# Weight subtractions of the state-space and router stage moved from GpSimd to Vector, gates computed directly behind the slot matrices

## The chip, the core and the metric

The kernel runs on one core of one Trainium2 chip. The metric is the device time of one execution in microseconds (us). Five engines work side by side, each through its own list of instructions in order: TensorE (PE: matrix products; PEld is its loading of weights), VectorE (DVE), ScalarE (ACT), GpSimd (POOL) and SyncE (SP), which here only issues transfers. An instruction waits for others by semaphores, and whatever stands behind it on its engine waits with it.

## The reference

Two decoder layers over 256 tokens with D = 1024, everything in float32. Layer 0 is attention and a dense SwiGLU. The change lies in layer 1: a state-space layer with a gated output, then a router that sends each token to two of eight expert SwiGLUs.

```python
def _s5_layer(x, norm_g, w_in, ...):
    u = _rms_norm(x, norm_g) @ w_in
    ...                                   # complex diagonal scan over the tokens, giving y
    z = gelu(y + d_skip * u) @ w_glu
    return x + z[..., :D_MODEL] * sigmoid(z[..., D_MODEL:])

def _moe_swiglu_layer(x, norm_g, w_router, w_gate, w_up, w_down):
    xt = _rms_norm(x, norm_g)
    logits = xt @ w_router
    top_vals, top_idx = lax.top_k(logits, 2)
    gates = softmax(top_vals)
    ...                                   # gather the tokens of each expert
    y_e = (silu(xb @ w_gate[e]) * (xb @ w_up[e])) @ w_down[e]
    return x + sum over the two experts of gate * y_e
```

## The kernel before, in words

**Weights.** Almost all of the time goes into large products with weights that come from memory in blocks. For most of them each float32 factor is split into a rounded part (high) and what is left (low), and a product is made of three matmuls: high by high, high by low, low by high (`mm3`, L248, its matmuls on L250 to L252). A weight block of 128x2048 arrives in a raw buffer in two halves of 128x1024. `half()` (L207) prepares one: ScalarE casts it to `wh` (L221), then one subtraction `wl = raw - wh` (L222) follows on the engine that `self.sub` names, or that the caller gives. The pair (wh, wl) lies in a ring of six slots, of which one is given up at L1445, so that five are left for the rest of the kernel. `take` and `takek` (L233, L244) hand pairs to the matmuls and make new ones so many ahead. When both halves of a raw buffer are split, `drop` returns the buffer, and `fetch` issues the next block's transfer on SyncE's queue (L184, L187). So a subtraction also sets when the next block may start to arrive. Experts 1, 3, 5 and 7 have at most 64 tokens; their products read the raw weights in plain float32 (L717, L751) and need no pairs.

**Order.** There is no scheduler in this part: each engine runs its instructions in the order in which the Python code emits them. In `s5_and_moe` (L1206) this is:

1. `s5_rows` gives the rows transposed and their sums of squares; `rsqrt` (L255 to L276) makes the norm factor `r` on Vector by a chain of tiny operations; the line behind it sets `self.sub = nc.gpsimd`, and `takek` makes two more pairs.
2. `project` multiplies by w_in. The eviction by ScalarE (L1230) takes `r` as its scale, and Vector transposes the result into the layout for the states (L1231); `enter` (L1274) is the next product on it. `chain` is the scan on Vector, a few of its products are on GpSimd (L1256).
3. `glu` (L1345) multiplies by w_glu; `gate(n)` (L1392, its sigmoids on L1395) and `residual(n, b)` (L1397) form h + z * sigmoid(z') for column half n and token block b; `rows` (L1403) forms `xn`, the rows times the gain; `rows_T` (L1407) transposes them on TensorE and ScalarE copies them out (L1412); `logits` (L1418) adds a column half's share of the router's logits.
4. The half n = 1 ends the stage: `self.split()` (two halves of weights, on GpSimd), the residuals, the transposes, the logits, then `squares` (L333, on ScalarE over whole rows, for the second norm factor) and one more `self.half(nc.gpsimd)`.
5. The router on Vector: maximum and index (L1477, L1478), `sel` (one-hot choice), `ss`, two small matmuls for the places, `posm` (L1485).
6. `experts` (L1603) runs a list of steps for expert 0. Step 0 makes the slot matrix `S` (L1579); `rows_rest` makes `xn` of column half 1 and drops the buffer "sa"; `weights` (L1493) is the second rsqrt and the two sigmoids of the top two logits, the gates; steps 2 and 3 gather the tokens by a product with `S` (L1598) and evict it (ScalarE L1600, then a subtraction on Vector). The first expert's products follow. At its fourth chunk `count()` (L1507) runs on Vector: some 25 tiny operations that order the experts by their number of tokens.

The helper `tt` (L1210) records every plain Vector operation of this stage, so these share one line and are told apart by tiles: `h` residual, `sg`/`gh` gates, `xn` rows, `sel` choice, `wy` evicted tokens.

Of the kernel before, what the change touches and what calls it, by code (L numbers as in the profile page):

```python
# [8 lines left out]
F32 = mybir.dt.float32  # L9
# [4 lines left out]
AF = mybir.ActivationFunctionType  # L14
ALU = mybir.AluOpType
# [3 lines left out]
P = 128  # L19
SEQ = 256  # L20
D = 1024
# [119 lines left out]
class Net:  # L141
# [185 lines left out]
    def squares(self, scr, act):  # L327

        nc = self.nc
        ssq = self.sm.tile([P, 2], F32, tag="ssq", name="ssq")  # L330
        for b in range(2):
            if b in act:
                nc.scalar.activation(scr[b], self.h[:, b], AF.Square, accum_out=ssq[:, b:b + 1])  # L333
            else:
                nc.vector.scalar_tensor_tensor(out=scr[b], in0=self.h[:, b], scalar=1.0, in1=self.h[:, b], op0=ALU.mult, op1=ALU.mult,
                                               accum_out=ssq[:, b:b + 1])
        return ssq
# [868 lines left out]
    def s5_and_moe(self):  # L1206
        nc, tc, ins = self.nc, self.tc, self.ins
        mm = nc.tensor.matmul
        v = nc.vector
        tt = lambda o, a, b, op: v.tensor_tensor(out=o, in0=a, in1=b, op=op)  # L1210
# [4 lines left out]
        xh, xl, ssq = self.srows  # L1215
        tt(ssq[:, 0], ssq[:, 0], ssq[:, 1], ALU.add)
        r = self.rsqrt(ssq[:, 0], 2, 1.0 / D)
        self.sub = nc.gpsimd
        W = self.takek(4, 1) + self.takek(4, 1)


# [170 lines left out]
        def gate(n):  # L1392
            for b in range(2):
                sg[b] = self.two(("sg", "gh")[b], 0)
                nc.scalar.activation(sg[b], pz[n, 1, b], AF.Sigmoid)  # L1395

        def residual(n, b, o=0, w=512):  # L1397
            c = slice(512 * n + o, 512 * n + o + w)
            s = sg[b][:, o:o + w]
            tt(s, s, pz[n, 0, b][:, o:o + w], ALU.mult)  # L1400
            tt(self.h[:, b, c], self.h[:, b, c], s, ALU.add)

        def rows(n, b):  # L1403
            c = slice(512 * n, 512 * n + 512)
            tt(xn[:, b, c], self.h[:, b, c], gb[:, c], ALU.mult)

        def rows_T(n, b, js=range(4)):  # L1407
            pt = pgu.tile([P, 4, P], F32, tag="gu", name="hpt")
            for j in js:
                k = 4 * n + j  # L1410
                nc.tensor.transpose(pt[:, j], self.h[:, b, k * P:(k + 1) * P], self.ident)
            nc.scalar.copy(hT[:, 4 * n + js[0]:4 * n + js[-1] + 1, blk[b]], pt[:, js[0]:js[-1] + 1])  # L1412
# [3 lines left out]
        def logits(n, b, js=range(4)):  # L1416
            for k in range(4 * n + js[0], 4 * n + js[-1] + 1):
                mm(pl[b], hT[:, k, blk[b]], self.wrg[:, k], start=(k == 0), stop=(k == KD - 1))  # L1418

        gate(0)  # L1420
        Wg.append(self.takek(4, 1))
        for b in range(2):
# [6 lines left out]
            rows_T(0, b)  # L1429
        for b in range(2):  # L1430
            logits(0, b)
        gate(1)
        Wg.append(self.takek(4, 1))
        glu(1, 0, 0, range(4))
# [8 lines left out]

        self.ahead = 4
        self.drop(self.ring.pop(0))  # L1445
        self.split()
        residual(1, 0)
        rows_T(1, 0)
        for o in range(2):
            pz[1, 0, 1] = last[o]  # L1450
            residual(1, 1, 256 * o, 256)
            rows_T(1, 1, range(2 * o, 2 * o + 2))
        for b in range(2):
            logits(1, b)
        self.sub = v
        ssq = self.squares([self.sa[:, 0]] * 2, (0, 1))
        self.half(nc.gpsimd)


        iota = self.cst[:, C_IO:C_IO + P + 1]  # L1460
# [31 lines left out]

        def weights():  # L1493

            r = self.rsqrt(ssq, 2, 1.0 / D)
            nc.scalar.activation(self.sm.tile([P, 1], F32, tag="cf", name="cf"), self.ones[:, 0:1], AF.Sigmoid)
            v.tensor_copy(GR[:, NE], r)
            dg = mo.tile([P, 2, 2], F32, name="dg")
            tt(dg[:, 0], mx[:, :, 0], mx[:, :, 1], ALU.subtract)
            tt(dg[:, 0], dg[:, 0], r, ALU.mult)  # L1500
            nc.scalar.activation(dg[:, 1], dg[:, 0], AF.Sigmoid, scale=-1.0)
            nc.scalar.activation(dg[:, 0], dg[:, 0], AF.Sigmoid)
            for s in range(2):
                tt(sel[:, s], sel[:, s], dg[:, s].unsqueeze(2).to_broadcast([P, 2, NE]), ALU.mult)
            tt(GR[:, 0:NE].rearrange("p e b -> p b e"), sel[:, 0], sel[:, 1], ALU.add)
# [205 lines left out]

            self.ffn([job(e) for e in range(NE)], g1, pgu)

        def rows_rest():
            for b in range(2):
                rows(1, b)
            self.drop((self.sl, "sa"))

        experts((0, rows_rest, weights, 2, 3), True)

        def over():

# [80 lines left out]
```

## Time and profile before

| | us |
|---|---|
| median of three runs (1299.54 to 1300.69) | 1299.7 |
| the profiled execution | 1299.78 |
| its span on the core | 1297.7 |
| TensorE busy | 1263.9 |
| VectorE busy | 829.0 |
| ScalarE busy | 634.9 |
| GpSimd busy | 205.2 |

The span runs from the first to the last instruction of the core; 2.1 us of the profiled execution lie around it. The mean granted clock of TensorE is 0.992 of full speed. All times below count from the start of the span; the stage of the change lies between 376 and 470 us. A row of the timeline gives start, duration, engine, line, operation, out<-in with sizes, the number of instructions taken together, and in brackets the idle time just before and what ended it. A row of the windows gives for a stretch its length and each engine's busy time with the number of instructions, then the granted clock, the share of the 16 DMA engines' time and the rate. A row of the groups gives the number, the busy time and the mean ns of one.

### The profile page before, as it was taken

To read this page: it belongs to the slowest core of one execution; us is meant where nothing else is said; L and a number is where in the kernel's file an instruction comes from. 1 tells how busy PE (TensorE), PEld (TensorE's weight loads), DVE (VectorE), ACT (ScalarE), POOL (GpSimd) and SP (SyncE) were. 2 spreads that over 40 slices of the span, in tenths; PEclk is the share of its full clock that TensorE was granted. 3 is DMA by queue.
4 is the path that set the end of the run, shared out by engine and by line. 5 is a ranking of instruction groups with operands and counts; after the bars stand their busy time and mean duration, and the time that the engine had idled before them with its cause. 6 is when DMAs were issued, how large, how long until landed. Compare 5 with 4: busy or idle time off the path is not lost.

```text
span 1297.7 us, 18489 instructions
## 1 busy us (share of the span) xinstructions
PE 1263.9 (97%) x6862; PEld 918.6 (71%) x6862; DVE 829.0 (64%) x1102; ACT 634.9 (49%) x825; POOL 205.2 (16%) x295
## 2 busy tenths in 40 slices
PE   8999999999998799999999999999999999999997
PEld 8867999999987688863458884356886345888433
DVE  7876869666777699861079982138985107998201
ACT  6665544444443378751067771046875106777100
POOL 1841994012815400000000000000000000000000
PEclk9999999999999799999999999999999999999999
DMA  8504653654446569999999999999999999999996
GB/s 313 215 7 176 250 180 136 218 182 176 162 163 247 224 246 376 359 369 393 420 418 417 417 419 413 420 417 417 418 418 418 419 418 418 418 418 418 414 419 239
DMA packets 66370, 421.23 MB, mean 325 GB/s; under 512 B 7504, under 2 KB 8784, under 8 KB 21472
## 3 DMA queue, kind: packets, MB, share of 16 engines
q1 hardware_dynamic: 65088, 418.15, 81.1%
q10 hardware_dynamic: 1008, 1.27, 0.3%
q8 instruction: 56, 0.92, 0.3%
q0 software_dynamic: 176, 0.56, 0.1%
q14 instruction: 42, 0.34, 0.1%
HBM read 418.89 MB, written 1.05 MB: 324 GB/s over the span
## 4 chain that ended last, share of the span: by engine, by line


## 5 line engine op out<-in xcount | busy, mean ns | idle before, releaser
L222 DVE TENSOR_TENSOR wl<-raw,wh 128x1024 fp32r<-128x1024 f32 (+1 forms) x445 | 533.5, 1235 | 103.1 <-ACT wh L221 90.3
L221 ACT CAST wh<-raw 128x1024 fp32r<-128x1024 f32 (+1 forms) x456 | 467.5, 1046 | 177.7 <-PE dn L252 62.7
L717 PE MATMUL pgu<-raw,we 128*64 128x512 f32 x896 | 203.6, 596 | 0.0
L250 PE MATMUL pgu<-wh,wy 128*128 128x512 f32 x448 | 178.2, 398 | 0.0
L251 PE MATMUL pgu<-wl,wy 128*128 128x512 f32 x448 | 174.7, 390 | 0.6 <-DVE wl L222 0.6
L252 PE MATMUL pgu<-wh,wy 128*128 128x512 f32 x448 | 174.8, 390 | 0.0
L717 PEld LDWEIGHTS pgu<-raw,we 128*64 128x64 f32 x896 | 61.0, 137 | 115.5 <-issue 114.0
L250 PE MATMUL pgu<-dxh,wh 128*128 128x256 f32 x448 | 127.3, 284 | 0.5 <-DVE h L679 0.5
L252 PE MATMUL pgu<-dxh,wl 128*128 128x256 f32 x448 | 126.8, 283 | 0.0
L251 PE MATMUL pgu<-dxl,wh 128*128 128x256 f32 x448 | 126.8, 283 | 0.0
L250 PE MATMUL dn<-wh,gh 128*128 128x512 f32 x280 | 109.8, 392 | 0.0
L252 PE MATMUL dn<-wh,gl 128*128 128x512 f32 x280 | 109.1, 390 | 0.0
L251 PE MATMUL dn<-wl,gh 128*128 128x512 f32 x280 | 109.0, 389 | 0.0
L751 PE MATMUL dn<-raw,gh 128*64 128x512 f32 x448 | 102.2, 593 | 0.5 <-ACT gh L737 0.5
L250 PEld LDWEIGHTS pgu<-wh,wy 128*128 128x128 f32 x448 | 84.2, 188 | 23.8 <-issue 4.7
L252 PEld LDWEIGHTS pgu<-wh,wy 128*128 128x128 f32 x448 | 84.1, 188 | 18.2
L251 PEld LDWEIGHTS pgu<-wl,wy 128*128 128x128 f32 x448 | 84.2, 188 | 17.4 <-DVE wl L222 1.0
L737 ACT COPY gh<-pgt 128x256 f32<-128x256 f32 x28 | 10.4, 372 | 163.7 <-PE pgt L735 163.7
L728 DVE TENSOR_TENSOR sg<-pgu,sg 64x512 f32<-64x512 f32 x28 | 19.4, 693 | 110.9 <-ACT sg L727 110.9
L250 PEld LDWEIGHTS pgu<-dxh,wh 128*128 128x128 f32 x448 | 85.9, 192 | 1.1 <-DVE h L679 0.7
L251 PEld LDWEIGHTS pgu<-dxl,wh 128*128 128x128 f32 x448 | 86.0, 192 | 0.3
L252 PEld LDWEIGHTS pgu<-dxh,wl 128*128 128x128 f32 x448 | 85.9, 192 | 0.0
(419 smaller groups left out, 1615.9 us busy)
## 6 DMA issues: line engine op xcount, KB each, us to landing
raw<-in_wm_dram SPq DMA_DIRECT2D x292, 1024.0 KB, 15.0
raw<-in_wm_dram SPq DMA_DIRECT2D x88, 512.0 KB, 15.0
raw<-in_wd_dram SPq DMA_DIRECT2D x42, 1024.0 KB, 5.0
raw<-in_wqkv_dram SPq DMA_DIRECT2D x6, 1024.0 KB, 6.6
raw<-in_wo_dram SPq DMA_DIRECT2D x4, 1024.0 KB, 5.9
raw<-in_wglu_dram SPq DMA_DIRECT2D x4, 1024.0 KB, 5.0
raw<-in_ws_dram SPq DMA_DIRECT2D x2, 1024.0 KB, 4.7
raw<-in_wc_dram SPq DMA_DIRECT2D x4, 416.0 KB, 6.7
```

The source lines that it names most:

```text
L221: self.nc.scalar.copy(wh, w)
L222: (sub or self.sub).tensor_tensor(out=wl, in0=w, in1=wh.bitcast(F32), op=ALU.subtract)
L250: mm(out, sh, mh, start=start, stop=False)
L251: mm(out, sh, ml, start=False, stop=False)
L252: mm(out, sl, mh, start=False, stop=stop)
L717: nc.tensor.matmul(pg[64 * j:64 * j + 64], x(k), W[j][0][k % 4], start=(k == 0), stop=(k == KD - 1))
L728: v.tensor_tensor(out=sg[:64], in0=pg[64:], in1=sg[:64], op=ALU.mult)
L737: nc.scalar.copy(g, pt)
L751: nc.tensor.matmul(job["acc"][64 * n:64 * n + 64], gts[0][:, k], W[n][0][k], start=(f == 0 and k == 0), stop=(f == NF - 1 and k == 3))
```

## The change

- `self.sub = nc.gpsimd` is deleted, so every subtraction `wl` of the stage goes to Vector, at the place in the order where `half()` is called: two directly behind the first rsqrt, four in front of `residual(0, ...)`, two in front of `residual(1, ...)`.
- The explicit `self.split()` in front of `residual(1, 0)` and the `self.half(nc.gpsimd)` behind the squares are removed. In their place three `self.half` stand in the first expert's list of steps: behind step 0, behind step 2 and behind step 3. The number of pairs that are made before the first expert's fourth chunk stays the same.
- The squares for the second norm factor are made in column halves on ScalarE: half 0 behind `logits(0, ...)` and in front of `gate(1)`, half 1 behind `logits(1, ...)`. `weights` adds the two sums first.
- `xn` of column half 1 is made in front of `logits(1, ...)`, not behind `S`; the buffer "sa" is dropped directly behind the second half of the squares.
- `weights` stood behind `rows_rest` and in front of step 2 and now stands behind one `half` and in front of step 2.

```diff
@@ s5_and_moe
         r = self.rsqrt(ssq[:, 0], 2, 1.0 / D)
-        self.sub = nc.gpsimd
         W = self.takek(4, 1) + self.takek(4, 1)
...
+        ssq = self.sm.tile([P, 2, 2], F32, tag="ssq4", name="ssq4")
+
+        def squares(n):
+            c = slice(512 * n, 512 * n + 512)
+            for b in range(2):
+                nc.scalar.activation(self.sa[:, 0, c], self.h[:, b, c], AF.Square, accum_out=ssq[:, n, b:b + 1])
+
         gate(0)
...
         for b in range(2):
             logits(0, b)
+        squares(0)
         gate(1)
         Wg.append(self.takek(4, 1))
         glu(1, 0, 0, range(4))
...
         self.drop(self.ring.pop(0))
-        self.split()
         residual(1, 0)
         rows_T(1, 0)
...
         for b in range(2):
+            rows(1, b)
+        for b in range(2):
             logits(1, b)
-        self.sub = v
-        ssq = self.squares([self.sa[:, 0]] * 2, (0, 1))
-        self.half(nc.gpsimd)
+        squares(1)
+        self.drop((self.sl, "sa"))
...
         def weights():
-            r = self.rsqrt(ssq, 2, 1.0 / D)
+            tt(ssq[:, 0], ssq[:, 0], ssq[:, 1], ALU.add)
+            r = self.rsqrt(ssq[:, 0], 2, 1.0 / D)
...
-        def rows_rest():
-            for b in range(2):
-                rows(1, b)
-            self.drop((self.sl, "sa"))
-
-        experts((0, rows_rest, weights, 2, 3), True)
+        experts((0, self.half, weights, 2, self.half, 3, self.half), True)
```

The lines of the changed kernel are one lower than before from L1219 on, and up to eight higher from the new function on.

The first place is Vector's list behind the first rsqrt (the last two rows of its chain, then the transposes of the projection; `sg` and `gx` are the evicted projections, `sa` their transposed form).

```order
 L271 SCALAR_TENSOR_TENSOR rt<-rr,rm 128x1 x2
 L276 SCALAR_TENSOR_TENSOR rr<-rt,rr 128x1 x2
-L1231 STREAM_TRANSPOSE sa<-sg 128x8x32
-L1231 STREAM_TRANSPOSE sa<-gx_4140 128x8x32
-L1231 STREAM_TRANSPOSE sa<-sg 128x8x32
+L222 TENSOR_TENSOR wl<-raw,wh 128x1024 x2
+L1230 STREAM_TRANSPOSE sa<-sg 128x8x32
+L1230 STREAM_TRANSPOSE sa<-gx_4140 128x8x32
+L1230 STREAM_TRANSPOSE sa<-sg 128x8x32
```

Two subtractions of weights now stand on Vector between the norm factor and the transposes.

The second place is Vector's list in the router, from the last choice to the start of the second rsqrt (`posm` the places, `S` the slot matrix, `rx` the first tile of the rsqrt).

```order
 L1210 TENSOR_TENSOR ss<-sel 128x16
-L1485 SCALAR_TENSOR_TENSOR posm<-dn_4697,ss 128x16
-L1579 TENSOR_SCALAR S<-cst,posm 128x128 x2
-L1210 TENSOR_TENSOR xn<-h,sa 128x512 x2
-L259 TENSOR_SCALAR rx<-ssq 128x2
+L1492 SCALAR_TENSOR_TENSOR posm<-dn_4689,ss 128x16
+L1587 TENSOR_SCALAR S<-cst,posm 128x128 x2
+L222 TENSOR_TENSOR wl<-raw,wh 128x1024
+L1210 TENSOR_TENSOR ssq_4513<-ssq_4513 128x2
+L259 TENSOR_SCALAR rx<-ssq_4513 128x2
```

The two `xn` have gone to a place further ahead, and one weight subtraction and the sum of the squares stand between `S` and the rsqrt.

The third place is ScalarE's list from the copies of the transposed rows (half 0) to the cast behind the squares, before:

```order
L1412 COPY wy_4509<-hpt 128x4x128 x2
L1395 ACTIVATE sg<-dn_4533 128x512
L1395 ACTIVATE gh<-dn_4546 128x512
L221 CAST wh<-raw 128x1024 x4
L1412 COPY wy_4509<-hpt 128x4x128
L1412 COPY wy_4509<-hpt 128x2x128 x2
L333 ACTIVATE sa,ssq<-h 128x1024 x2
L221 CAST wh<-raw 128x1024
```

and now:

```order
L1411 COPY wy_4509<-hpt 128x4x128 x2
L1424 ACTIVATE sa,ssq_4513<-h 128x512 x2
L1394 ACTIVATE sg<-dn_4534 128x512
L1394 ACTIVATE gh<-dn_4547 128x512
L221 CAST wh<-raw 128x1024 x2
L1411 COPY wy_4509<-hpt 128x4x128
L1411 COPY wy_4509<-hpt 128x2x128 x2
L1424 ACTIVATE sa,ssq_4513<-h 128x512 x2
L221 CAST wh<-raw 128x1024
```

Two squares of half width now stand ahead of the gates, two casts fewer stand behind them, and the squares behind the copies are half as wide.

## The prediction

> **What bounds the kernel now.** I read the busy line of the page first, then windows around the stage, then the groups of L222, then the timeline at each place where TensorE stands still.
>
> ```profile
> PE 1263.9 (97%) x6862; PEld 918.6 (71%) x6862; DVE 829.0 (64%) x1102; ACT 634.9 (49%) x825; POOL 205.2 (16%) x295
> core 0: us, PE busy (x) PEld busy (x) DVE busy (x) ACT busy (x) POOL busy (x), PEclk, DMA share, GB/s
> 386.00:407.00 21.00, 16.21 (x160) 14.42 (x160) 20.71 (x46) 4.89 (x7) 10.30 (x14) 1.00 0.41 154
> 411.00:425.00 14.00, 14.00 (x66) 11.56 (x65) 7.04 (x7) 6.99 (x10) 10.09 (x4) 1.00 0.89 329
> 434.20:439.70 5.50, 1.49 (x8) 1.08 (x9) 4.92 (x5) 1.33 (x3) 4.70 (x2) 0.82 0.85 337
> 439.70:443.20 3.50, 3.44 (x18) 3.38 (x17) 0.43 (x4) 3.20 (x6) 0.00 (x0) 0.50 1.00 332
> 447.10:452.70 5.60, 5.60 (x33) 5.60 (x33) 4.61 (x25) 0.88 (x3) 0.00 (x0) 0.62 0.53 187
> 452.70:463.00 10.30, 9.72 (x51) 7.79 (x49) 7.54 (x32) 7.49 (x9) 0.00 (x0) 1.00 0.28 103
> 600.00:700.00 100.00, 99.07 (x472) 53.40 (x472) 45.26 (x49) 38.22 (x48) 0.00 (x0) 1.00 1.01 418
> ```
>
> TensorE is busy 97% of the span, so only its gaps and slow stretches can go. Vector sets the pace in 386 to 407 (20.71 of 21). In 434.2 to 439.7 TensorE works 1.49 of 5.5 while Vector and GpSimd are both almost full. The next stretch runs at a granted clock of 0.50.
>
> ```profile
> L222 DVE TENSOR_TENSOR wl<-raw,wh 128x1024 fp32r<-128x1024 f32 x10 | 11.7, 1218 | 1.2 <-ACT wh L221 1.2
> L222 POOL TENSOR_TENSOR wl<-raw,wh 128x1024 fp32r<-128x1024 f32 x11 | 27.5, 2524 | 43.9 <-PE dn L252 25.8 <-ACT wh L221 18.1
> ```
>
> Eleven subtractions, 2.52 us each on GpSimd, 1.22 us on Vector. The question is what Vector's own work loses while GpSimd makes one.
>
> **First rsqrt, and the two subtractions behind it.**
>
> ```profile
> 377.13 2.46 DVE L276 SCALAR_TENSOR_TENSOR rr<-rt,ri 128x1 f32<-128x1 f32 x2
> 377.18 4.75 POOL L222 TENSOR_TENSOR wl<-raw,wh 128x1024 fp32r<-128x1024 f32 x2 [25.80 <-PE dn L252]
> 379.51 2.56 DVE L271 SCALAR_TENSOR_TENSOR rt<-rr,rm 128x1 f32<-128x1 f32 x2
> 382.69 0.47 ACT L1230 ACTIVATE sg<-dn,rr 128x256 f32<-128x256 f32 x1 [4.64 <-DVE rr L276]
> 384.14 1.97 PE L1274 MATMUL pe<-sa,we 128*128 128x128 f32 x16 [1.21 <-issue]
> 449.98 0.27 DVE L276 SCALAR_TENSOR_TENSOR rr<-rt,rr 128x1 f32<-128x1 f32 x2
> ```
>
> Operations on one column, 0.27 us a pair at 449.98 with GpSimd idle, take 2.46 and 2.56 while GpSimd subtracts. Without that r is ready 4.5 earlier, at 382.69 - 4.5 = 378.2. The two subtractions then stand ahead of the transposes: 378.2 + 2 x 1.22 = 380.7. From the end of ScalarE's eviction (383.16) to TensorE's start lie 1.0, mostly transposes, so they are done at 381.7. TensorE works until 384.14 - 1.21 = 382.93 and then goes on at once: **-1.2**. The chain behind it fills Vector and nothing is added there, so the gain carries through; were Vector's chain held up by something the trace doesn't show, the gain would be 0.
>
> **Residual of half 0, with four subtractions ahead.**
>
> ```profile
> 417.74 2.00 ACT L221 CAST wh<-raw 128x1024 fp32r<-128x1024 f32 x2
> 425.19 1.03 PE L1411 MATMUL hpt<-cst,h 128*128 128x128 f32 x8
> ```
>
> The last cast ends at 419.74; the third subtraction starts at 418.75, the fourth ends at 421.2, and then come two products (0.7 each) and two adds (0.65) to 423.9. TensorE wants h at 425.19 and is full in 411 to 425, so this costs **0** with 1.3 us of cover. If the adds stay at 2.1, as some do beside GpSimd now, it costs about 1.6.
>
> **Residual of half 1.**
>
> ```profile
> 427.74 2.96 ACT L221 CAST wh<-raw 128x1024 fp32r<-128x1024 f32 x3
> 431.38 0.69 DVE L1210 TENSOR_TENSOR sg<-sg,pz 128x512 f32<-128x512 f32 x1 [4.96 <-PE pz L1345]
> 432.11 2.11 DVE L1210 TENSOR_TENSOR h<-h,sg 128x512 f32<-128x512 f32 x1
> 434.58 2.13 DVE L1210 TENSOR_TENSOR h<-h,gh 128x256 f32<-128x256 f32 x1
> 437.07 2.12 DVE L1210 TENSOR_TENSOR h<-h,gh 128x256 f32<-128x256 f32 x1
> 439.24 0.69 PE L1411 MATMUL hpt<-cst,h 128*128 128x128 f32 x2 [1.98 <-DVE h L1210]
> 440.24 1.06 ACT L333 ACTIVATE sa<-h 128x1024 f32<-128x1024 f32 x1
> 447.13 1.29 DVE L1210 TENSOR_TENSOR xn<-h,sa 128x512 f32<-128x512 f32 x2
> ```
>
> Three adds take 2.1 each, whether 512 or 256 wide; a clean one of 512 takes 1.29 / 2 = 0.65, and I take 0.35 for 256. Ahead of them stands more now: squares(0) delays ScalarE by about 1.3 (two of half width, 0.53 each by the row of the full one, and 0.2 for reading the sums), so the first cast runs from 429.1 to 430.1, the second to 431.1. Two subtractions follow, to 432.6, instead of the start at 431.38. Then 0.69 + 0.65 + 0.41 + 0.35 + 0.41 + 0.35 = 2.9, with 0.2 of gaps: 435.7 instead of 439.24, **-3.5**. On SyncE the transfers that waited for GpSimd's subtractions wait for Vector's, which end earlier.
>
> **Logits.**
>
> ```profile
> 426.46 1.95 PE L1418 MATMUL dn<-kp,wy 128*128 128x8 f32 x16 [0.24 <-ACT wy L1412]
> 439.72 3.42 PE L1418 MATMUL dn<-kp,wy 128*128 128x8 f32 x16
> ```
>
> The same sixteen matmuls take 1.95 at full clock and 3.42 in the stretch at 0.50, which follows 5.5 us with 1.49 of work. With the adds shortened, the last gap shrinks to under 2 us and the stretch is about 60% busy, so I take full clock: **-1.5**, or 0 if it still drops. The two xn, now ahead of the logits on Vector, take 1.3 while TensorE makes these logits: nothing.
>
> The Trainium skill, "TensorE: Matmul & The Clock Gate", Part 1, says that the clock goes to half after an idle window of about 3.4 us and back after a busy one. The row shows 0.50 behind a stretch that was never idle for that long (1.49 of 5.5 busy), so the trace is harsher than the rule; by the rule the term is -1.5, by the row alone it may be 0.
>
> **Router, and the gather.**
>
> ```profile
> 443.67 2.36 DVE L1210 TENSOR_TENSOR sel<-cst,ix 128x16 f32<-128x16 f32 x2
> 447.08 5.85 PE L1598 MATMUL dn<-S,xn 128*128 128x128 f32 x32 [0.59 <-DVE S L1579]
> 448.34 0.16 DVE L259 TENSOR_SCALAR rx<-ssq 128x2 f32<-128x2 f32 x1
> 451.22 0.26 DVE L1210 TENSOR_TENSOR sel<-sel,dg 128x16 f32<-128x16 f32 x2 [0.51 <-ACT dg L1502]
> 451.70 0.69 DVE L1210 TENSOR_TENSOR wy<-dn,wy 128x512 fp32r<-128x512 f32 x1
> 456.63 0.15 DVE L1590 COPY gs<-dn 128x2 f32<-128x2 f32 x1
> 461.70 6.90 DVE L222 TENSOR_TENSOR wl<-raw,wh 128x1024 fp32r<-128x1024 f32 x6
> 462.99 0.50 PE L251 MATMUL pgu<-wl,wy 128*128 128x512 f32 x1 [0.58 <-DVE wl L222]
> ```
>
> `sel` takes 2.36 beside GpSimd's last subtraction, a like pair 0.26 alone: **-2.1**. So the gather starts 1.2 + 3.5 + 1.5 + 2.1 = 8.3 earlier, at 438.8.
>
> From there to the seventh weight pair, the first that TensorE waits for, it is now 462.99 - 447.08 = 15.9. After: 0.1, one subtraction 1.2, the sum of the squares 0.2, rsqrt and gates 3.4 (448.34 to 451.70), eviction 0.7: 5.6; then 0.4 for a cast, 1.2, the second eviction 0.7, 1.2, and the sixth pair 1.2: 10.3. `count()` takes 5.1 (456.63 to 461.70) and the seventh subtraction 1.2: 16.6. **+0.7** (0 if TensorE's own work up to that pair, 15.1 before its wait, gets longer by as much; +2.9 if a cast waits for a ring slot and comes late with its subtraction, 1.0 + 1.2, since the evictions and all of `count()` are queued behind it on Vector).
>
> **The sum.** -1.2 + 0 - 3.5 - 1.5 - 2.1 + 0.7 = -7.6. Does it reach the end? From 600 on the transfers fill the DMA engines (1.01, 418 GB/s), so the stream must start earlier as well.
>
> ```profile
> SPq L187 <- DVE wl L222: 29.8, 10, 7.9
> ```
>
> It can: in 452.7 to 463 the share is 0.28, and this row, SyncE's waits between 430 and 500, says that its issues stand behind Vector's subtractions. These shift with the stage, and the stream with them. The profiled execution becomes 1299.78 - 7.6 = 1292.2; it lies 0.08 over the median, so the forecast is **1292.1**. That the gates now come "in front of the evictions" adds nothing: `weights` stood ahead of step 2 before.
>
> **The rivals.**
>
> *The clock still drops in the router.* For it: 0.50 behind a stretch that was partly busy. Against: a shorter gap. 1292.1 + 1.5 = **1293.6**, chance 0.15.
>
> *Vector's queue is the bound in the first expert*, by a cast that waits for a slot: +2.9 instead of +0.7, **1294.3**; chance 0.06. Against: one slot of the five is free each time TensorE ends a pair, and the cast has been early so far (1.2 us of waiting in all for ten subtractions).
>
> *The stream of weights does not move*, because the last bytes are bound from further ahead: **1299.7**, no change; chance 0.08. Against: the share of 0.28.
>
> *Slower: the stalls are not GpSimd's.* If the tiny operations and the adds stay long for a reason of their own, the subtractions come on top of Vector's path: two ahead of the transposes, 382.69 + 2.4 to start them instead of 383.2, +1.9; the residual 432.6 instead of 431.38, +1.1; and +0.7. That is +3.7: **1303.4**, chance 0.05. It decides from the point where the rsqrt chain without GpSimd still takes over about 4 us. Against it: 0.27 at 449.98.
>
> The Trainium skill, "Perfetto Trace Analysis", Optimizing Scalar/DVE Operations, speaks against the change: where Vector is saturated, offloading to Scalar or even GpSimd may make sense, though it adds that Vector and GpSimd share a read port, so it might not help. Here 11 x 1.22 = 13.4 us go onto Vector, but none falls into the one stretch that is full (20.71 of 21), so the rule would cost its 13.4 only if that were so everywhere.
>
> **How the numbers follow.** Forecast 0.66, clock 0.15, queue 0.06, stream 0.08, slower 0.05. Faster than 0.2% (2.6 us, about what a measurement of this kernel can tell from no change) holds the first three: 0.87; same 0.08; slower 0.05. The range goes from 1289.5 to 1296.0. Its lower end is the forecast without the +0.7 and with the residual's start not put off by the squares (431.4 instead of 432.6), 1290.2, less 0.7 for the spread of runs; its upper end is the clock and the queue together, 1295.8. It leaves out 0.13 and a little of the forecast's own spread.
>
> **What would show it.** In the profile of the changed kernel: L276 and L271 behind the first rsqrt at 0.3 a pair and no gap of 1.21 ahead of L1273; adds of half 1 at 0.65 and 0.35; the last transposes at about 434.5; the logits at 1.95 with a clock of 1.00; `sel` at 0.26; the gather at 438.8 and the seventh pair 16.6 behind it; no subtraction on GpSimd. I am wrong if adds stay near 2.1 with GpSimd idle, if the last weights land no earlier than now, or if the seventh pair comes later than 18 behind the gather.

## The result and the profile after

The changed kernel took 1290.07 us (median of four runs, 1289.86 to 1291.47) against 1299.62 for the kernel before: ratio 0.993, 95% interval 0.9914 to 0.9946. A second set of five runs, beside 21 of the kernel before, gave 1291.43 against 1299.55, ratio 0.9932 (0.9918 to 0.9945). The span of the profiled execution went from 1297.7 to 1288.1.

The busy line of the page and the group of Vector's subtractions between 374 and 462 us, after:

```profile
PE 1260.8 (98%) x6862; PEld 915.1 (71%) x6862; DVE 826.5 (64%) x1114; ACT 635.4 (49%) x829; POOL 178.2 (14%) x284
L222 DVE TENSOR_TENSOR wl<-raw,wh 128x1024 fp32r<-128x1024 f32 x23 | 27.0, 1220 | 8.9 <-ACT wh L221 8.9
```

GpSimd lost its eleven subtractions (27 us). Vector made them at 1.22 each, 13.4 in all, and is yet 2.5 us less busy than before: what it took on is less than what it had spent held up.

The timeline after the first rsqrt:

```profile
377.50 0.27 DVE L276 SCALAR_TENSOR_TENSOR rr<-rt,ri 128x1 f32<-128x1 f32 x2
378.61 2.36 DVE L222 TENSOR_TENSOR wl<-raw,wh 128x1024 fp32r<-128x1024 f32 x2
381.25 0.40 DVE L1230 STREAM_TRANSPOSE sa<-gx 128x256 f32<-128x256 f32 x1
383.15 1.90 PE L1273 MATMUL pe<-sa,we 128*128 128x128 f32 x16
```

The small operations take 0.27 a pair, the two subtractions stand behind them, and TensorE's row has no idle time in brackets any more. The rest of the stage, from the residual of half 1 to the seventh weight pair:

```profile
427.52 2.36 DVE L222 TENSOR_TENSOR wl<-raw,wh 128x1024 fp32r<-128x1024 f32 x2 [5.17 <-ACT wh L221]
429.80 0.68 DVE L1210 TENSOR_TENSOR sg<-sg,pz 128x512 f32<-128x512 f32 x1
430.51 0.69 DVE L1210 TENSOR_TENSOR h<-h,sg 128x512 f32<-128x512 f32 x1
431.57 0.42 DVE L1210 TENSOR_TENSOR h<-h,gh 128x256 f32<-128x256 f32 x1
432.36 0.42 DVE L1210 TENSOR_TENSOR h<-h,gh 128x256 f32<-128x256 f32 x1
433.12 1.93 PE L1417 MATMUL dn<-kp,wy 128*128 128x8 f32 x16
435.57 0.26 DVE L1210 TENSOR_TENSOR sel<-cst,ix 128x16 f32<-128x16 f32 x2
436.53 0.48 DVE L1587 TENSOR_SCALAR S<-cst,posm 128x128 f32<-128x128 f32 x2
436.87 6.07 PE L1606 MATMUL dn<-S,xn 128*128 128x128 f32 x32 [0.59 <-DVE S L1587]
444.55 2.36 DVE L222 TENSOR_TENSOR wl<-raw,wh 128x1024 fp32r<-128x1024 f32 x2 [0.15 <-ACT wh L221]
446.82 0.15 DVE L1598 COPY gs<-dn 128x2 f32<-128x2 f32 x1
451.91 6.90 DVE L222 TENSOR_TENSOR wl<-raw,wh 128x1024 fp32r<-128x1024 f32 x6
453.19 0.50 PE L251 MATMUL pgu<-wl,wy 128*128 128x512 f32 x1 [0.80 <-DVE wl L222]
```

The adds take 0.69 and 0.42, the logits 1.93, the choice 0.26; the gather stands at 436.87 (438.8 was foretold) and the seventh pair 16.3 behind it.

Executions reach this stage up to 1.4 us apart, so two profiles are compared from one mark: the sum of the squares on Vector (`ssq<-ssq`, at 376.19 before and 376.56 after). The table counts every start from it, except for the end of the last add. It is made from the timeline of each profile, and the later kernels stand in it too; the last column is TensorE's first product for the output (`po<-Y,ST`), 1288.77 before and 1279.07 after.

| | first product on the transposed input | transposes, half 0 | last add, its end | gather | seventh pair | output product |
|---|---|---|---|---|---|---|
| before | 7.95 | 49.00 | 63.00 | 70.89 | 86.80 | 912.58 |
| before, second profile | 7.95 | 48.75 | 62.74 | 70.63 | 86.21 | 912.30 |
| after | 6.59 | 45.94 | 56.22 | 60.31 | 76.63 | 902.51 |
| after, second profile | 6.59 | 47.52 | 58.96 | 62.98 | 79.05 | 905.18 |
| all subtractions on Vector, old order | 6.58 | 45.92 | 59.45 | 67.07 | 83.00 | 908.71 |
| new order, eight on GpSimd | 7.95 | 48.99 | 60.32 | 65.16 | 81.22 | 907.08 |
| first two on GpSimd | 7.95 | 47.39 | 57.68 | 61.69 | 78.30 | 904.55 |
| last two on GpSimd | 6.58 | 45.97 | 57.29 | 62.56 | 79.32 | 905.23 |
| three idle two-input operations | 6.57 | 45.93 | 60.12 | 65.92 | 82.83 | 909.01 |
| one of these, eight idle memsets | 6.59 | 45.94 | 57.92 | 63.71 | 79.83 | 906.04 |
| half ahead of the router on GpSimd | 6.57 | 47.57 | 57.86 | 63.68 | 80.68 | 906.58 |
| gates first | 6.57 | 47.55 | 57.82 | 61.83 | 78.28 | 904.30 |

From the sum of the squares to the output product the first pair of profiles differs by 912.58 - 902.51 = 10.07, the second by 912.30 - 905.18 = 7.12. What differs between the two profiles of the changed kernel is the granted clock, below.

### The profile page after: what moved, and what is told of

Same layout as the page of the kernel before. It is cut to its first block, busy times and chain, and to the rows that moved or that the text cites. A ratio compares the mean times of both kernels' runs of the same rounds, so it can differ in the third digit from the quotient of the medians.

```text
span 1288.1 us, 18482 instructions
## 1 busy us (share of the span) xinstructions
PE 1260.8 (98%) x6862; PEld 915.1 (71%) x6862; DVE 826.5 (64%) x1114; ACT 635.4 (49%) x829; POOL 178.2 (14%) x284
## 4 chain that ended last, share of the span: by engine, by line
## 5 line engine op out<-in xcount | busy, mean ns | idle before, releaser
L222 DVE TENSOR_TENSOR wl<-raw,wh 128x1024 fp32r<-128x1024 f32 (+1 forms) x456 | 546.4, 1235 | 110.8 <-ACT wh L221 97.7
```

The costliest lines, as they stand in the source:

```text
L222: (sub or self.sub).tensor_tensor(out=wl, in0=w, in1=wh.bitcast(F32), op=ALU.subtract)
```

## Experiments: engine or order

**All subtractions on Vector, old order** (the kernel before):

```diff
-        self.sub = nc.gpsimd
...
-        self.half(nc.gpsimd)
+        self.half(v)
```

> The kernel before with all eleven subtractions on Vector at the places where they stood, and nothing else moved. Theory (GpSimd's subtractions stall Vector, but the place of Vector's own decides how much comes back): the first rsqrt's small operations go back to 0.3 a pair and give 1.1; in front of the residual of half 1 now stand four subtractions, and the cast of the fourth waits for a ring slot (433.5 in the profile of before), so Vector starts the residual at about 435.8 and ends it at 438.9 instead of 439.2: 0.3; in the router the one subtraction stands ahead of the maximum and ends at 444.7: 0.2. Sum -1.6: 1298.1, or 1296.5 if the clock also stays full in 407 to 411. Rival 1 (the engine alone is the whole gain): 1290. Rival 2 (the new order alone is the gain): 1299.7.

Measured: 1297.42, ratio 0.9986 (0.9977 to 0.9995), between the two expected values.

```profile
430.15 1.05 ACT L221 CAST wh<-raw 128x1024 fp32r<-128x1024 f32 x1 [2.80 <-PE dn L1344]
432.37 0.68 DVE L1210 TENSOR_TENSOR sg<-sg,pz 128x512 f32<-128x512 f32 x1
435.90 3.42 PE L1417 MATMUL dn<-kp,wy 128*128 128x8 f32 x16
439.71 1.23 DVE L222 TENSOR_TENSOR wl<-raw,wh 128x1024 fp32r<-128x1024 f32 x1 [4.35 <-ACT wh L221]
```

The adds are short (0.69 and 0.42), but the fourth cast waits 2.80 for a ring slot that TensorE frees, Vector stands still behind it, and the logits run at half clock behind that gap. From the transposes to the last add this order needs 13.53, the kernel before 14.00: 0.5 of the 3.7 that the change gained there. In the router the subtraction now waits ahead of the maximum, and from the last add to the gather it is 7.62 against 7.89. So the engine alone gives the term of the first rsqrt (7.95 to 6.58) and little else.

**New order, eight subtractions on GpSimd again** (the changed kernel):

```diff
         r = self.rsqrt(ssq[:, 0], 2, 1.0 / D)
+        self.sub = nc.gpsimd
         W = self.takek(4, 1) + self.takek(4, 1)
...
+        self.sub = v
         squares(1)
```

> The changed kernel with the eight subtractions of the state-space stage on GpSimd again; the three in the list of the first expert stay on Vector, and the new order stays. Theory: +1.1 for the first rsqrt, +0.7 for the residual of half 1 (GpSimd's last subtraction ends at about 435, adds of 2.1 beside it), nothing in the router, and up to 1.5 each if the clock drops in 407 to 411 and at the logits: 1291.9 to 1295. Rival 1 (the engine alone is the gain): 1299.7. Rival 2 (the order alone is the gain): 1290.1.

Measured: 1294.24, ratio 0.9956 (0.9942 to 0.9969), inside the range. The first product is at 7.95 again, the last add ends 11.33 behind the transposes (after: 10.28; before: 14.00), and the router is as fast as after but for the logits, which took 2.68, in part at half clock. The engine alone gave 2.2 of 1299.6, the new order 5.4, both together 8.1 to 9.6: neither rival is the whole. That both together give 0.5 to 2.0 more than the sum of the two is not shown, since the intervals reach 1.2 to 2.1 us to either side. Nor is this kernel the order alone: three of the eleven subtractions stay on Vector in it, and one of them, put back on GpSimd, holds up the router by 1.6 (below). What the squares in halves and the earlier `xn` give by themselves no kernel here shows.

**Only the first two, or only the last two, on GpSimd** (the changed kernel; the same two lines around the first, or around the last `takek` of the stage):

```diff
+        self.sub = nc.gpsimd
         Wg.append(self.takek(4, 1))
+        self.sub = v
```

> The changed kernel with only the two subtractions behind the first rsqrt on GpSimd again. Theory: L276 and L271 take 2.5 a pair, r comes 4.5 later, TensorE has its gap of 1.2 ahead of L1273 again: +1.1, 1291.2; 1292.8 if the clock then drops in 407 to 411 as it did before. Rival (the small operations were slow for a reason of their own): they stay at 0.3 and r is as early as in the changed kernel, 1290.1 or, since Vector has two subtractions less there, no change.

> The changed kernel with only the two subtractions in front of the residual of half 1 on GpSimd again. Theory: they run there from 427.5 to 432.6; the residual starts 1.1 earlier, but its adds that fall beside them take 2.1 instead of 0.7, and its end comes 0.5 later: 1290.6. Rival (GpSimd does not hold Vector): the adds stay at 0.7 and 0.4 and the residual ends 1.1 earlier, 1289.0.

Measured: 1293.9, ratio 0.9956 (0.9942 to 0.9969), and 1293.08, ratio 0.9951 (0.9937 to 0.9965). The timeline with the first two on GpSimd:

```profile
376.33 2.45 DVE L276 SCALAR_TENSOR_TENSOR rr<-rt,ri 128x1 f32<-128x1 f32 x2
376.37 4.75 POOL L222 TENSOR_TENSOR wl<-raw,wh 128x1024 fp32r<-128x1024 f32 x2 [25.79 <-PE dn L252]
383.34 1.86 PE L1275 MATMUL pe<-sa,we 128*128 128x128 f32 x15 [1.21 <-issue]
```

The stall and the gap of 1.21 are back with these two subtractions alone: 1.36 at the first product. That disposes of the rival in which the small operations are slow for a reason of their own. At the output product it is 2.0: of the rest, 0.3 falls between the gather and the seventh pair, where the gather takes 6.36 in place of 6.07, and 0.4 behind that. The median is above the expected 1291.2 to 1292.8; why stays open. The timeline with the last two on GpSimd:

```profile
427.01 5.19 POOL L222 TENSOR_TENSOR wl<-raw,wh 128x1024 fp32r<-128x1024 f32 x2 [23.55 <-ACT wh L221]
428.87 1.11 DVE L1210 TENSOR_TENSOR h<-h,sg 128x512 f32<-128x512 f32 x1
430.35 2.14 DVE L1210 TENSOR_TENSOR h<-h,gh 128x256 f32<-128x256 f32 x1
432.85 0.42 DVE L1210 TENSOR_TENSOR h<-h,gh 128x256 f32<-128x256 f32 x1
433.61 3.10 PE L1417 MATMUL dn<-kp,wy 128*128 128x8 f32 x16
```

Counted from the mark, the residual starts 1.1 earlier (at 428.15 in this profile) and still ends 1.1 later, as the first two adds wait for GpSimd; the third, behind its end at 432.2, takes 0.42. The logits then take 3.10 at half clock, which was not in the expectation: 2.7 at the output product instead of 0.5.

## Experiments: what holds Vector

Two kernels put idle work on GpSimd that nothing else needs. It is released by the last cast ahead of the residual of half 1; its result goes to a dead part of "sa".

```diff
         Wg.append(self.takek(4, 1))
+        o = self.pairs[-1][0].bitcast(F32)
+        dmy = self.sa[:, 0, 0:512].bitcast(BF16)
+        nc.gpsimd.tensor_tensor(out=dmy, in0=o, in1=o, op=ALU.subtract)
+        for _ in range(2):
+            nc.gpsimd.tensor_tensor(out=dmy, in0=o, in1=o, op=ALU.subtract)
```

In the second kernel the loop is `for _ in range(8): nc.gpsimd.memset(dmy, 0.0)`.

> The changed kernel with three idle GpSimd operations added (128x1024, two inputs from SBUF, result unused), released by the last cast in front of the residual of half 1, at 428.5. Nothing of Vector depends on them. Theory (a GpSimd operation with two inputs holds back Vector's operations with two inputs from SBUF until it ends): they run to about 436; the second subtraction and the adds beside them take 2 to 2.5 each, products that read PSUM keep 0.7 and 0.4; the residual ends about 4 later and the clock may drop: 1294 to 1296. Rival (no such hold): 1290.1, adds at 0.7 and 0.4.

> As the one with three idle operations, but only the first has two inputs; then eight idle memsets of 128x1024 follow, which read nothing. Theory (it is the reading that holds Vector): only the second weight subtraction is held, to about 431, and the adds behind it are at 0.7 and 0.4: +1.3, 1291.4. Rival (any work on GpSimd holds Vector): adds of 1 to 2 as with three idle operations, 1294.

Measured: 1296.26, ratio 0.9977 (0.9968 to 0.9986), and 1292.8, ratio 0.9953 (0.994 to 0.9967). The first lies 0.3 above its expected range, and its residual ends 3.9 later than after, as expected. With three two-input operations:

```profile
428.50 1.98 POOL L1443 TENSOR_TENSOR sa<-wh 128x1024 bf16<-128x1024 f32 x1 [24.48 <-ACT wh L221]
430.57 5.05 POOL L1445 TENSOR_TENSOR sa<-wh 128x1024 bf16<-128x1024 f32 x2
432.20 1.67 DVE L1210 TENSOR_TENSOR h<-h,sg 128x512 f32<-128x512 f32 x1
433.79 0.41 DVE L1210 TENSOR_TENSOR gh<-gh,pz 128x256 f32<-128x256 f32 x1
434.23 1.67 DVE L1210 TENSOR_TENSOR h<-h,gh 128x256 f32<-128x256 f32 x1
436.26 0.42 DVE L1210 TENSOR_TENSOR h<-h,gh 128x256 f32<-128x256 f32 x1
```

With memsets:

```profile
430.11 8.01 POOL L1445 MEMSET sa<- 128x1024 bf16 x8
431.76 0.69 DVE L1210 TENSOR_TENSOR h<-h,sg 128x512 f32<-128x512 f32 x1
432.82 0.43 DVE L1210 TENSOR_TENSOR h<-h,gh 128x256 f32<-128x256 f32 x1
433.61 0.42 DVE L1210 TENSOR_TENSOR h<-h,gh 128x256 f32<-128x256 f32 x1
```

The reader should look at the widths: an add of 512 and one of 256 both take 1.67 beside a GpSimd operation that reads. They end at 433.87 and 435.90, 0.5 and 0.3 behind the end of a GpSimd operation, so their time goes by that end and not by their size. Beside eight memsets, with GpSimd just as busy, the same adds take 0.69 and 0.43. The product between them (`gh<-gh,pz`), whose second input is in PSUM, takes 0.41 either way. So it is not GpSimd's being busy that holds Vector, but its operations that read; and they hold Vector's adds, whose inputs are both in SBUF, and not the product with an input in PSUM. The memset kernel lies 1.4 above its expected 1291.4, mostly because its logits ran at half clock (3.42).

The Trainium skill, "SBUF — State Buffer", Who interferes with whom, says that Vector and GpSimd share one pair of ports under an exclusive lock, and that a Vector operation with two SBUF inputs needs it against a GpSimd operation that reads SBUF. These two runs agree with it: 1.67 against 0.43.

**The half ahead of the router on GpSimd, and the gates first** (the changed kernel):

```diff
         self.drop((self.sl, "sa"))
+        self.half(nc.gpsimd)
...
-        experts((0, self.half, weights, 2, self.half, 3, self.half), True)
+        experts((0, weights, 2, self.half, 3, self.half), True)
```

and, for the other kernel, only the list `(0, weights, self.half, 2, self.half, 3, self.half)`.

> The changed kernel with the first of the three subtractions of the expert's list back on GpSimd, directly behind the squares, as it was before. Theory: the choice operation takes 2.4 again and the gather comes 2.1 later, but Vector has 1.2 less between the gather and the seventh weight pair: +0.9, 1291.0. Rival (Vector's queue behind the gather is what counts, not the gather): -1.2, 1288.9.

> The changed kernel with the gates ahead of the first of the three subtractions, directly behind the slot matrices. Theory: the gates and the first eviction come 1.2 earlier, but TensorE's gather ends at the same time, and the seventh pair stands behind the same sum of Vector's work: 0, 1290.1. Rival (the place of the gates sets the first expert's start): -1.2, 1288.9.

Measured: 1292.63, ratio 0.995 (0.9936 to 0.9964), and 1290.67, ratio 0.9933 (0.9919 to 0.9947). The timeline of the first:

```profile
436.30 2.35 POOL L222 TENSOR_TENSOR wl<-raw,wh 128x1024 fp32r<-128x1024 f32 x1 [33.68 <-DVE sel L1210]
436.94 2.09 DVE L1588 TENSOR_SCALAR S<-cst,posm 128x128 f32<-128x128 f32 x2
438.83 6.78 PE L1607 MATMUL dn<-S,xn 128*128 128x128 f32 x32 [2.14 <-DVE S L1588]
```

The subtraction came later than thought, behind the choice, and held the slot matrix instead (2.09 against 0.48): the gather came 1.6 later, counted from the second maximum, by the same mechanism at another operation. The 1.2 that Vector had less behind the gather brought nothing: the gather took 6.78 and the seventh pair stands 17.0 behind it, not 15.1. So Vector's queue alone does not set that stretch. The durations of the gather show what does. In the seven profiles of the new order in the table whose gather took 5.89 or more, the seventh pair stands 10.2 behind the gather's end (10.22 to 10.25). In the two with a shorter gather (5.47 in the second profile of after, 5.32 with eight on GpSimd) it stands 16.07 and 16.06 behind the gather's start. The later of the two counts: the gather's end and 10.2, or Vector's queue, 16.1 from the gather's start. The median of this kernel is 1.6 above the expected 1291.0; its profile has the drop of the clock ahead of the transposes (next section), which makes 1.6 of its 4.1 at the output product. The gates' place is worth nothing that shows: 16.45 from gather to seventh pair against 16.32. That is what the prediction said of the gates.

## Experiments: the clock

> The changed kernel once more, unchanged, for a second profile beside the others on one chip. Theory (the half clock that stood in 407 to 411 in the profile of before and not in that of the changed kernel comes and goes from run to run and is no work of the change): the median ratio to before stays near 0.993, and the residual of half 0 ends either 45.9 or 47.6 behind the sum of the squares. Rival (the change removes it): 45.9 in every profile of the changed kernel.

> The kernel before once more, unchanged, for a second profile. Theory (the half clock behind the gap at 404 comes and goes): the transposes of half 0 stand 47.3 or 49.0 behind the sum of the squares, 1299.6 in the median. Rival: 49.0 always.

Both kernels are unchanged. Measured: 1291.43, ratio 0.9932 (0.9918 to 0.9945), and 1299.65, ratio 1.0001 (0.9991 to 1.0011). The second profile of the changed kernel, windows (granted clock third from the right):

```profile
core 0: us, PE busy (x) PEld busy (x) DVE busy (x) ACT busy (x) POOL busy (x), PEclk, DMA share, GB/s
406.00:407.00 1.00, 1.00 (x14) 0.92 (x10) 1.00 (x2) 0.00 (x0) 0.00 (x0) 0.57 0.97 410
425.00:426.00 1.00, 1.00 (x11) 1.00 (x11) 0.00 (x0) 0.97 (x4) 0.00 (x0) 1.00 0.00 0
427.00:428.00 1.00, 1.00 (x4) 0.80 (x3) 0.00 (x0) 1.00 (x3) 0.00 (x0) 0.50 0.00 0
```

The kernel before, first profile:

```profile
407.00:411.00 4.00, 4.00 (x30) 3.50 (x27) 2.43 (x3) 0.60 (x1) 0.00 (x0) 0.58 0.82 274
```

In the first profile of the changed kernel the same stretches were at full clock, and the clock fell later, at the end of the logits:

```profile
405.50:411.00 5.50, 5.50 (x48) 4.71 (x49) 3.62 (x6) 2.53 (x4) 0.00 (x0) 1.00 0.76 265
426.00:431.00 5.00, 5.00 (x34) 4.53 (x33) 3.45 (x4) 2.43 (x4) 0.00 (x0) 1.00 0.11 15
437.00:441.00 4.00, 4.00 (x19) 4.00 (x20) 3.47 (x21) 0.29 (x2) 0.00 (x0) 0.50 1.01 350
```

Same program, same gaps, another place of the half clock: 1.6 up to the transposes, 2.7 up to the last add and the end. Of the twelve profiles in the table six had the drop at 404 to 411 (both of before, the second of after, and three others). From the first product to the transposes these six need 40.8 to 41.1, the other six 39.3 to 39.4; the old order and the new, with and without subtractions on GpSimd, stand in both groups. So for the changed kernel the theory stands: the change does not remove the drop, and the rival falls. For the kernel before it is not settled, as both its profiles have the drop. That the drop comes and goes there too is suggested, not shown, by the mean clock of its 21 runs: 0.993 or 0.994 in the eight up to 1298.39 us, 0.992 in the thirteen from 1298.85 on.

The Trainium skill, "TensorE: Matmul & The Clock Gate", Part 1, calls the window in which activity is watched free-running, and says that the moment at which the clock rises therefore varies from run to run. Here it is the fall that varies: the granted clock was 0.57 in 406 to 407 in one profile of the changed kernel and 1.00 in the other.

The last two kernels put nine idle matmuls into TensorE's gap of 2.4 ahead of the second half of the states, in the changed kernel and in the kernel before:

```diff
         Wg.append(self.takek(4, 0))
+        for _ in range(9):
+            mm(self.bank(3), yh[:, 0, blk[0]], Wg[0][0][0][:, 0:512], start=True, stop=True)
         states(1)
```

> The changed kernel with nine idle matmuls (128x512, result unused) in TensorE's gap of 2.4 at 403 to 405.5, ahead of the second half of the states. Theory: the clock stays at 1.00 in 403 to 411 in every run, the time is at the fast end of the changed kernel's own runs, 1289.5, and the runs lie closer together. Rival (a run's clock there does not reach the end): the same median and spread as the changed kernel.

> The kernel before with the same nine idle matmuls in the same gap. Theory: the clock stays full there; 1.7 less than the runs that have the drop, so 1298 to 1299.6 by how often they have it. Rival (the drop costs nothing at the end): 1299.6.

Measured: 1292.01, ratio 0.9944 (0.993 to 0.9958), and 1300.24, ratio 1.0007 (0.9998 to 1.0016). The timeline of the changed kernel with the filling:

```profile
401.24 4.84 PE L1366 MATMUL dn<-wh,Y 128*128 128x512 f32 x9
406.01 1.97 PE L1312 MATMUL dn<-wy,H 128*64 128x128 f32 x32
```

The clock stayed at 1.00 in 401 to 411 in both, but both times are above the expected (1289.5, and 1298 to 1299.6). The nine took 4.84, twice the gap of 2.4: each opens a new tile in the same bank, and its weight load waited for the one before (3.1 us in eight waits). That put the states off: the transposes stand 47.80 behind the mark, 1.9 later than in the profile of after without a drop. What the clock gave the filling took. The runs lay closer together in the kernel before (1299.3 to 1300.74, against 1297.41 to 1300.37 without the filling), not in the changed kernel (1290.77 to 1293.12). This pair does not settle what the drop costs at the end.

## Why the prediction was right

The direction, the mechanism and the range hold; 1290.07 is 2.0 below the forecast of 1292.1. By its steps, in the first pair of profiles (differences from the table; the logits are split off by the second maximum, at 443.18 before and 435.08 after):

| step | forecast | measured |
|---|---|---|
| first rsqrt, no gap ahead of the first product | -1.2 | -1.36 |
| up to the transposes of half 0 (residual 0, cover) | 0 | -1.70 |
| residual of half 1 | -3.5 | -3.72 |
| logits | -1.5 | -1.69 |
| router | -2.1 | -2.11 |
| gather to seventh pair | +0.7 | +0.41 |
| from there to the output product | 0 | +0.10 |
| sum | -7.6 | -10.07 |

The five terms of the sum lie within 0.3. **The step that failed is one left out**: the prediction set the stretch up to the transposes at 0, and it gave 1.70, because the half clock of 407 to 411 in the profile of before (4.0 us of work at 0.58, a loss of 1.7) was absent in that of after. The working of this term was sound in itself: the adds of half 0 ended 1.36 ahead of the transposes, 1.3 of cover were foretold. The repeat shows this to be a matter of the run: there the transposes came 1.23 earlier, for which the 1.36 of the first rsqrt accounts, and the residual gave 2.55 in place of 3.72, as TensorE made the products ahead of it at half clock. Its sum is 7.12. The forecast of 7.6 lies between the two profiles, and a single pair of profiles cannot do better than that here. That the median of 1290.07 still lies inside the range is in part luck: the lower end was made from two other terms, no +0.7 and a residual not put off by the squares, and neither came about (+0.41, and a start 7.3 behind the transposes, where 7.4 were worked out).

*The clock rival* had the right price and the wrong place. In the first profile of after the logits ran at full clock (1.93) and the drop came at their end and slowed the gather (6.07); in four of the experiments, where the residual ended later, it came earlier and the logits took 3.1 to 3.4.

*Gather to seventh pair*: the number held (16.3 against 16.6), its working only half. Vector's queue alone, worked out at 10.3 up to `count()` and 16.6 in all, takes 9.71 and 16.07, as the second profile of after shows. In the first the gather, at half clock, took 6.07, and its end set the stretch, 0.25 above that. Two readings of the prediction are off by little and change no term of the sum: TensorE's own work up to that pair was 15.3 before, not 15.1, and the residual of the slower rival would have come 1.2 later, not 1.1.

*The stream of weights* moved with the stage: the output product came 9.7 earlier on the span's own time, and the transfers ended earlier too: before, the DMA share is 0.98 in 1270 to 1280 and 0.15 in the ten us behind; after, it is 0.98 in 1260 to 1270 and 0.17 in the ten us behind. SyncE's waits between 420 and 490, after:

```profile
SPq L187 <- DVE wl L222: 41.2, 11, 11.0
```

Its issues stand behind Vector's subtractions, and none stands behind GpSimd's any more. *The slower rival*, stalls that were not GpSimd's, fell with the first row of the timeline and with the kernel in which two subtractions alone brought them back. The rule of the Trainium skill beside it ("Perfetto Trace Analysis", Optimizing Scalar/DVE Operations: taking work off a saturated Vector may make sense) did not bind: Vector's busy time went from 829.0 to 826.5.

That the place in the order counts beside the engine was in the prediction's working of the residual (two subtractions ahead of it, not four): with the engine alone, 0.5 of the 3.7 was to be had there.

## What to carry to other kernels

Where one engine may hold another up, look for operations whose time does not depend on their size (2.1 for 512 and for 256 columns, 2.5 for one column): that excess, not the work moved, is what the first engine costs the second, and moving 13.4 us onto a busy engine can make it less busy. Move the work and place it in the same step: behind what the next engine waits for, where its own input is ready; here the engine alone was worth about a quarter of the gain. And before a term of 1 to 2 us is read from one profile, take a second of the same kernel: here the clock alone moved the end of the stage by 2.7.

## What the runs showed of the hardware that was not expected

- The granted clock fell to 0.50 at 426.6 in the second profile of after while TensorE was busy 1.00 in every microsecond of 425 to 428; the work before it was the transposes and the sixteen logits matmuls of 8 columns. In the kernel before with the filling it was 0.58 in 428 to 429 and 0.50 in 429 to 431, again with TensorE busy 1.00 and behind the same work, and without any gap over 0.3 since 408. In the first profile of after the clock fell at about 434.7, at the end of such work, with gaps of up to 0.3 ahead of it. In the kernel before without the filling it stayed at 1.00 from 426 to 430. That narrow matmuls bring the drop about is an argument from these places, not shown by a run of its own.
- Building the slot matrix, one tensor input and a scalar per partition, was held by GpSimd's subtraction as well (2.09 against 0.48), and so were the rsqrt's operations on one column (2.45 against 0.27).
